# A top-2 expert dispatch on one core: one store fewer at the start, other load sizes, and a last store of the first half cut in two

## The chip, the cores and the metric

The kernel runs on one core of a Trainium2 chip. The metric is the device time of one execution in microseconds (us), the median of several runs. TensorE does nothing here. Four parts of the core matter: VectorE (DVE in the profile), ScalarE (ACT), the 16 DMA engines that carry all data between HBM and the on-chip memory, and SyncE (SP), which issues DMAs in program order and waits for semaphores before it does. ScalarE can issue DMAs too, on a queue of its own.

## The reference

There are 16 x 1024 = 16384 tokens with 512 float32 values each, and 8 router logits for each token. A softmax over the logits, its two largest values, and a division of these two by their sum give two weights a token; the output is the token's row times each weight.

```python
probs = probs / np.sum(probs, axis=-1, keepdims=True)
topk_indices = np.argsort(probs, axis=-1)[..., -k:]
topk_probs = np.take_along_axis(probs, topk_indices, axis=-1)
topk_probs = topk_probs / np.sum(topk_probs, axis=-1, keepdims=True)
x_expanded = x[:, :, np.newaxis, :].repeat(k, axis=2)
return (x_expanded * topk_probs[..., np.newaxis]).astype(np.float32)
```

So 33.6 MB of x are read and 67.1 MB are written. With two experts the weights are the sigmoids of plus and minus the difference of the two largest logits, and the kernel computes them so.

## The kernel before

Each of the 128 partitions holds M = 128 tokens, called rows here; one row in all partitions is 128 x 512 x 4 bytes = 262,144 bytes to load, and twice that, two half-rows, to store. The rows are worked in two groups of 65 and 63 (`GROUPS`, L16). `xs` has room for 65 rows of x. `osp` (`OSP`, L38) has room for 18 rows of output; its last three rows serve first as the place of the logits and as scratch for `top2_weights` (L41 to L68).

For each group the kernel issues its loads from SP (L111, L112) in the sizes of `LOADS` (L20): 6, 28 and 31 rows, then 32 and 31. Behind the first load, of 6 rows, come the two small loads of logits (L105, L106), and the weights of all rows are computed once, on DVE and with two sigmoids on ACT (L67, L68), into `WA`.

Then come the stores of the group, from `STORES` (L23 to L37). An entry gives the number of rows, where the output rows are built, how many of them ACT computes, and the queue. DVE multiplies most rows in one instruction (L127), which reads each row of x once for each of its two weights; ACT does the others, one activation a half-row (L135). When all are done the entry's DMA is issued (L138). An output row is built in `osp`, or in `xs` itself, over rows of x that are used up. "x", 2 means that the 16 output rows lie over xs rows 2 to 33, while they are computed from rows 18 to 33, in ascending order, so that no row is overwritten before it is read.

What sets the order is therefore this. SP has one list: the loads of the first group (group 0 in the code), its stores as they come ready, then the loads of the second group, and the second group's stores. A DMA that reads or writes rows that another piece of work still uses waits for it, and so does everything behind it on SP. The first load of the second group fills xs rows 0 to 31, the second one rows 32 to 62; each waits for the stores of group 0 that still read those rows. Before the change the stores of the first group are these: 2 rows from `osp` issued from ACT's queue as soon as the first 6 rows and the weights are there ("the early store"); 16 rows from `osp`; 16 rows from xs rows 2 to 33; 16 rows from `osp` again, which waits until the earlier `osp` store has landed; 15 rows from xs rows 35 to 64. The first load of the second group has no row in common with the last of these.

```python
            {"SP": nc.sync, "ACT": nc.scalar}[queue].dma_start(o_v[g][:, r : r + n], og)
```

In the texts below the loads are called A (6 rows), B, C (first group) and D, E (second group); the four stores of 15 to 17 rows of the first group are S0 to S3 in the order of the list, those of the second group T0 to T3.

Of the kernel before, what the change touches and what calls it, by code (L numbers as in the profile page):

```python
# [1 line left out]

# [4 lines left out]

F32 = mybir.dt.float32
ALU = mybir.AluOpType
ACTF = mybir.ActivationFunctionType  # L10
P = 128
E = 8
D = 512


GROUPS = [65, 63]  # L16
M = sum(GROUPS)


LOADS = [[6, 28, 31], [32, 31]]  # L20


STORES = [  # L23
    [
        (2, ("osp", 0), 0, "ACT"),
        (16, ("osp", 2), 0, "SP"),
        (16, ("x", 2), 0, "SP"),
        (16, ("osp", 0), 4, "SP"),
        (15, ("x", 35), 0, "SP"),
    ],  # L30
    [
        (16, ("osp", 0), 1, "SP"),
        (16, ("x", 0), 0, "SP"),
        (16, ("osp", 0), 4, "SP"),
        (15, ("x", 33), 0, "SP"),
    ],
]  # L37
OSP = 18  # L38


def top2_weights(nc, scratch, logits, WA):  # L41

    used = [0]

    def cut(n):
        a = scratch[:, used[0] : used[0] + M * n].rearrange("p (m n) -> p m n", n=n)
        used[0] += M * n
        return a

    a, b = logits[:, :, 0:4], logits[:, :, 4:8]  # L50
    hi = cut(4)
    lo = b
    nc.vector.tensor_tensor(hi, a, b, op=ALU.max)  # L53
    nc.vector.tensor_tensor(lo, a, b, op=ALU.min)  # L54
    n = 4
    while n > 1:
        n //= 2
        a, b = hi[:, :, 0:n], hi[:, :, n : 2 * n]
        nhi, nlo, tmp = cut(n), cut(n), cut(n)
        nc.vector.tensor_tensor(tmp, lo[:, :, 0:n], lo[:, :, n : 2 * n], op=ALU.max)  # L60
        nc.vector.tensor_tensor(nlo, a, b, op=ALU.min)  # L61
        nc.vector.tensor_tensor(nlo, nlo, tmp, op=ALU.max)  # L62
        nc.vector.tensor_tensor(nhi, a, b, op=ALU.max)  # L63
        hi, lo = nhi, nlo
    dlt = cut(1)
    nc.vector.tensor_tensor(dlt, hi, lo, op=ALU.subtract)  # L66
    nc.scalar.activation(WA[:, :, 0], dlt[:, :, 0], ACTF.Sigmoid, scale=-1.0)  # L67
    nc.scalar.activation(WA[:, :, 1], dlt[:, :, 0], ACTF.Sigmoid, scale=1.0)  # L68


@with_exitstack
def kernel(
    ctx: ExitStack,
    tc: tile.TileContext,
    x: bass.AP,
    router_logits: bass.AP,
    k: bass.AP,
    out: bass.AP,
):
    nc = tc.nc  # L80
    N = x.shape[0] * x.shape[1]
    assert int(k) == 2 and router_logits.shape[-1] == E and x.shape[2] == D
    assert N == P * M
    xf = x.rearrange("b s d -> (b s) d")
    of = out.rearrange("b s k d -> (b s) k d")
    rf = router_logits.rearrange("b s e -> (b s) e")
    x_v, o_v, rl_v = [], [], []
    t0 = 0
    for n in GROUPS:
        t1 = t0 + P * n  # L90
        x_v.append(xf[t0:t1].rearrange("(p m) d -> p m d", p=P))
        o_v.append(of[t0:t1].rearrange("(p m) k d -> p m k d", p=P))
        rl_v.append(rf[t0:t1].rearrange("(p m) e -> p m e", p=P))
        t0 = t1

    pool = ctx.enter_context(tc.tile_pool(name="pool", bufs=1))
    xs = pool.tile([P, max(GROUPS), D], F32)
    osp = pool.tile([P, OSP, 2, D], F32)
    WA = pool.tile([P, M, 2], F32)

    logits = osp[:, OSP - 1].rearrange("p k d -> p (k d)").rearrange("p (m e) -> p m e", e=E)
    scratch = osp[:, OSP - 3 : OSP - 1].rearrange("p r k d -> p (r k d)")

    def load_logits():
        nc.sync.dma_start(logits[:, : GROUPS[0]], rl_v[0])  # L105
        nc.sync.dma_start(logits[:, GROUPS[0] :], rl_v[1])  # L106

    m0 = 0
    for g, G in enumerate(GROUPS):
        r = 0  # L110
        for n in LOADS[g]:  # L111
            nc.sync.dma_start(xs[:, r : r + n, :], x_v[g][:, r : r + n, :])  # L112
            if g == 0 and r < 6 <= r + n:
                load_logits()
                top2_weights(nc, scratch, logits, WA)
            r += n
        assert r == G
        r = 0
        for n, (home, a), by_act, queue in STORES[g]:
            if home == "x":  # L120
                og = xs[:, a : a + 2 * n, :].rearrange("p (r k) d -> p r k d", k=2)
            else:
                og = osp[:, a : a + n]
            v = n - by_act
            w = WA[:, m0 + r : m0 + r + n, :]
            if v:
                nc.vector.tensor_tensor(  # L127
                    og[:, :v],
                    xs[:, r : r + v, :].unsqueeze(2).to_broadcast([P, v, 2, D]),
                    w[:, :v].unsqueeze(3).to_broadcast([P, v, 2, D]),  # L130
                    op=ALU.mult,
                )
            for i in range(v, n):
                for c in range(2):
                    nc.scalar.activation(  # L135
                        og[:, i, c], xs[:, r + i, :], ACTF.Copy, scale=w[:, i, c : c + 1]
                    )
            {"SP": nc.sync, "ACT": nc.scalar}[queue].dma_start(o_v[g][:, r : r + n], og)  # L138
            r += n
        assert r == G  # L140
        m0 += G


# [1 line left out]
_INS = ['x', 'router_logits', 'k']  # L145
_OUTS = [((16, 1024, 2, 512), 'float32')]

_NUMBERS = {'k': 2}


# [26 lines left out]
```

## Time and profile before

| what | value |
|---|---|
| median of 3 runs | 239.16 us (239.15 to 239.52) |
| the profiled execution, its own time | 239.38 us |
| its span, first to last instruction | 237.6 us |
| DVE busy | 132.2 us, 56% |
| ACT busy | 13.2 us, 6% |
| bytes by DMA | 101.19 MB, mean 426 GB/s over the span |

The span is what the trace covers; 1.8 us of the execution lie outside of it. A row of the page with 40 digits cuts the span in 40 slices of 5.94 us; a digit is the busy share of a slice in tenths, and the row named DMA is the mean of the 16 DMA engines. In the view of windows the last two numbers of a row are the DMA share and the GB/s. Both count a transfer's packet where it starts, with its whole length and all its bytes, so a short window can show more than 1.00, and the quotient of the two columns, the rate while busy, says more than either. "SPq" and "ACTq" are instructions of the engines' queues: an issue, not the transfer. The "us to landing" of an issue runs from its issue to its completion and so holds the time that it stood behind earlier transfers.

### The profile page before, as it was taken

What the parts mean: (1) busy time and instruction counts of PE and PEld (TensorE: products, weight loads), DVE (VectorE), ACT (ScalarE), POOL (GpSimd) and SP (SyncE); (2) the same over time, 40 slices, a digit from 0 to 9 for tenths busy, and PEclk for the clock granted to TensorE, in tenths of its full rate; (3) what the DMA queues carried; (4) which work ended last, traced back from release to release, by engine and by line L of the source; (5) the groups of instructions that cost most, each with busy time, mean ns of one, the idle gap of its engine ahead of it and who ended that gap; (6) DMA issues with size and microseconds to landing.
All of it is one profiled execution on the core that took longest, in us unless ns stands there. A gap on an engine that the chain in (4) does not pass through costs nothing.

```text
span 237.6 us, 124 instructions
## 1 busy us (share of the span) xinstructions
DVE 132.2 (56%) x20; ACT 13.2 (6%) x21; POOL 0.2 (0%) x4
## 2 busy tenths in 40 slices
DVE  0640599999289999000000009999956999920000
ACT  2000000000080000000000001000006100000000
POOL 0000000000000000000000000000000000000000
DMA  7979989898989989899998989898989989897995
GB/s 265 541 338 488 408 386 535 348 530 353 496 386 441 441 353 530 353 508 414 414 519 353 508 370 502 353 519 353 496 386 419 463 353 530 353 530 342 496 445 217
DMA packets 2304, 101.19 MB, mean 426 GB/s; under 512 B 256, under 2 KB 384, under 8 KB 512
## 3 DMA queue, kind: packets, MB, share of 16 engines
q1 hardware_dynamic: 2160, 100.14, 97.7%
q10 hardware_dynamic: 144, 1.05, 1.0%
HBM read 34.08 MB, written 67.11 MB: 426 GB/s over the span
## 4 chain that ended last, share of the span: by engine, by line
DMA 48%; DVE 39%; SPq 1%; issue 0%; DVEq 0%
DMA xs<-in_x_dram 30%; DVE osp L127 25%; DMA out_dram<-osp 19%; DVE xs L127 14%; SPq L105 0%; SPq L106 0%; SPq L112 0%; SPq L138 0%; DVEq L127 0%
## 5 line engine op out<-in xcount | busy, mean ns | idle before, releaser
L127 DVE TENSOR_TENSOR osp<-xs,WA 128x12288 f32<-128x12288 f32 (+3 forms) x5 | 61.6, 12318 | 68.7 <-DMA xs<-in_x_dram 58.4
L127 DVE TENSOR_TENSOR xs<-xs,WA 128x16384 f32<-128x16384 f32 (+1 forms) x4 | 66.8, 16692 | 0.3
L135 ACT ACTIVATE osp<-xs,WA 128x512 f32<-128x512 f32 x18 | 11.4, 709 | 161.3 <-DMA out_dram<-osp 90.0
L53 DVE TENSOR_TENSOR osp<-osp 128x512 f32<-128x512 f32 x1 | 0.7, 692 | 8.2 <-DMA osp<-in_router_logits_dram 8.2
L67 ACT ACT_TABLE_LOAD x1 | 1.3, 1283 | 0.7 <-PEq L158 0.7
L67 ACT ACTIVATE WA<-osp 128x128 f32<-128x128 f32 x1 | 0.3, 316 | 10.1 <-DVE osp L66 10.1
L54 DVE TENSOR_TENSOR osp<-osp 128x512 f32<-128x512 f32 x1 | 0.7, 693 | 0.0
L60 DVE TENSOR_TENSOR osp<-osp 128x256 f32<-128x256 f32 (+1 forms) x2 | 0.7, 352 | 0.0
L62 DVE TENSOR_TENSOR osp<-osp 128x256 f32<-128x256 f32 (+1 forms) x2 | 0.7, 352 | 0.0
L63 DVE TENSOR_TENSOR osp<-osp 128x256 f32<-128x256 f32 (+1 forms) x2 | 0.7, 352 | 0.0
L61 DVE TENSOR_TENSOR osp<-osp 128x256 f32<-128x256 f32 (+1 forms) x2 | 0.7, 351 | 0.0
L66 DVE TENSOR_TENSOR osp<-osp 128x128 f32<-128x128 f32 x1 | 0.3, 292 | 0.0
L68 ACT ACTIVATE WA<-osp 128x128 f32<-128x128 f32 x1 | 0.3, 298 | 0.0
L158 POOL MEMSET const-bfloat16-1.0<- 128x1 bf16 x1 | 0.1, 102 | 0.0
L158 POOL MEMSET const-uint8-127<- 128x1 uint8 x1 | 0.1, 102 | 0.0
L158 POOL MEMSET const-float32-0.0<- 128x1 f32 x1 | 0.1, 99 | 0.2 <-issue 0.2
L158 POOL MEMSET const-float32-1.0<- 128x1 f32 x1 | 0.1, 99 | 0.0
## 6 DMA issues: line engine op xcount, KB each, us to landing
xs<-in_x_dram SPq DMA_DIRECT2D x2, 7936.0 KB, 40.8
out_dram<-xs SPq DMA_DIRECT2D x2, 7680.0 KB, 27.5
xs<-in_x_dram SPq DMA_DIRECT2D x1, 7168.0 KB, 24.2
xs<-in_x_dram SPq DMA_DIRECT2D x1, 1536.0 KB, 6.0
out_dram<-osp ACTq DMA_DIRECT2D x1, 1024.0 KB, 24.5
osp<-in_router_logits_dram SPq DMA_DIRECT2D x1, 260.0 KB, 6.2
osp<-in_router_logits_dram SPq DMA_DIRECT2D x1, 252.0 KB, 6.4
out_dram<-osp SPq DMA_DIRECT2D x4, 23.9
```

Source lines behind the costliest of these rows:

```text
L53: nc.vector.tensor_tensor(hi, a, b, op=ALU.max)
L54: nc.vector.tensor_tensor(lo, a, b, op=ALU.min)
L60: nc.vector.tensor_tensor(tmp, lo[:, :, 0:n], lo[:, :, n : 2 * n], op=ALU.max)
L61: nc.vector.tensor_tensor(nlo, a, b, op=ALU.min)
L62: nc.vector.tensor_tensor(nlo, nlo, tmp, op=ALU.max)
L63: nc.vector.tensor_tensor(nhi, a, b, op=ALU.max)
L66: nc.vector.tensor_tensor(dlt, hi, lo, op=ALU.subtract)
L67: nc.scalar.activation(WA[:, :, 0], dlt[:, :, 0], ACTF.Sigmoid, scale=-1.0)
L68: nc.scalar.activation(WA[:, :, 1], dlt[:, :, 0], ACTF.Sigmoid, scale=1.0)
L127: nc.vector.tensor_tensor(og[:, :v], xs[:, r : r + v, :].unsqueeze(2).to_broadcast([P, v, 2, D]), w[:, :v].unsqueeze(3).to_broadcast([P, v ...
L135: nc.scalar.activation(og[:, i, c], xs[:, r + i, :], ACTF.Copy, scale=w[:, i, c : c + 1])
L158: nc = _bacc.Bacc("TRN2", target_bir_lowering=False, num_devices=1)
```

## The change

The early store is gone from the list, and with it the entry for ACT's queue. The loads of the first group are 6, 29 and 30 rows. An entry of `LOADS` now also names the xs row where it begins (the same as before by running count), and an entry of `STORES` the xs row from which its rows are computed. The stores of the first group are 16, 16, 16 and 17 rows. S0 is built in `osp` from row 0 of it, with 2 rows by ACT; S1 over xs rows 0 to 31, from rows 16 to 31; S2 in `osp`, as the third store before; S3, 17 rows computed from xs rows 48 to 64, 4 of them by ACT, over xs rows 14 to 47. S3's DMA is cut in two: the first 29 half-rows (xs rows 14 to 42) and the last 5 (xs rows 43 to 47). The first load of the second group, rows 0 to 31, now has rows in common with S1 and with the first part of S3; the second load, rows 32 to 62, with both parts. The second group's tables are the same as before.

```diff
-LOADS = [[6, 28, 31], [32, 31]]
+LOADS = [[(6, 0), (29, 6), (30, 35)], [(32, 0), (31, 32)]]
 STORES = [
     [
-        (2, ("osp", 0), 0, "ACT"),
-        (16, ("osp", 2), 0, "SP"),
-        (16, ("x", 2), 0, "SP"),
-        (16, ("osp", 0), 4, "SP"),
-        (15, ("x", 35), 0, "SP"),
+        (16, 0, ("osp", 0), 2, "SP", 0),
+        (16, 16, ("x", 0), 0, "SP", 0),
+        (16, 32, ("osp", 0), 4, "SP", 0),
+        (17, 48, ("x", 14), 4, "SP", 5),
     ],
...
-        for n, (home, a), by_act, queue in STORES[g]:
+        for n, s, (home, a), by_act, queue, cut in STORES[g]:
...
-                    xs[:, r : r + v, :].unsqueeze(2).to_broadcast([P, v, 2, D]),
+                    xs[:, s : s + v, :].unsqueeze(2).to_broadcast([P, v, 2, D]),
...
-            {"SP": nc.sync, "ACT": nc.scalar}[queue].dma_start(o_v[g][:, r : r + n], og)
+            src = og.rearrange("p m k d -> p (m k) d")
+            dst = o_v[g][:, r : r + n].rearrange("p m k d -> p (m k) d")
+            for c0, c1 in ((0, 2 * n - cut), (2 * n - cut, 2 * n)):
+                if c0 < c1:
+                    {"SP": nc.sync, "ACT": nc.scalar}[queue].dma_start(
+                        dst[:, c0:c1], src[:, c0:c1]
+                    )
```

More of the change, by code (lines that the diff above doesn't have):

```diff
@@ L17 @@
 M = sum(GROUPS)
-LOADS = [[6, 28, 31], [32, 31]]
+LOADS = [[(6, 0), (29, 6), (30, 35)], [(32, 0), (31, 32)]]
 STORES = [
     [
-        (2, ("osp", 0), 0, "ACT"),
-        (16, ("osp", 2), 0, "SP"),
-        (16, ("x", 2), 0, "SP"),
-        (16, ("osp", 0), 4, "SP"),
-        (15, ("x", 35), 0, "SP"),
-    ],
-    [
[L32 to L35, printed above, removed]
+        (16, 0, ("osp", 0), 2, "SP", 0),
+        (16, 16, ("x", 0), 0, "SP", 0),
+        (16, 32, ("osp", 0), 4, "SP", 0),
+        (17, 48, ("x", 14), 4, "SP", 5),
+    ],
+    [
+        (16, 0, ("osp", 0), 1, "SP", 0),
+        (16, 16, ("x", 0), 0, "SP", 0),
+        (16, 32, ("osp", 0), 4, "SP", 0),
+        (15, 48, ("x", 33), 0, "SP", 0),
     ],
@@ L110 @@
         r = 0
-        for n in LOADS[g]:
-            nc.sync.dma_start(xs[:, r : r + n, :], x_v[g][:, r : r + n, :])
+        for n, s in LOADS[g]:
+            nc.sync.dma_start(xs[:, s : s + n, :], x_v[g][:, r : r + n, :])
             if g == 0 and r < 6 <= r + n:
@@ L135 @@
                     nc.scalar.activation(
-                        og[:, i, c], xs[:, r + i, :], ACTF.Copy, scale=w[:, i, c : c + 1]
+                        og[:, i, c], xs[:, s + i, :], ACTF.Copy, scale=w[:, i, c : c + 1]
                     )
-            {"SP": nc.sync, "ACT": nc.scalar}[queue].dma_start(o_v[g][:, r : r + n], og)
+            src = og.rearrange("p m k d -> p (m k) d")
[5 more added lines that the diff above has]
+                    )
             r += n
```

## The prediction, made before the changed kernel ran

> **What bounds the kernel now.** I read the page first, for who is busy.
>
> ```profile
> span 237.6 us, 124 instructions
> DVE  0640599999289999000000009999956999920000
> DMA  7979989898989989899998989898989989897995
> q1 hardware_dynamic: 2160, 100.14, 97.7%
> q10 hardware_dynamic: 144, 1.05, 1.0%
> ```
>
> DVE rests for long stretches; the DMA engines never do. Their packets fill 97.7% + 1.0% of 16 engines' span. SP's queue is q1; q10 is ACT's, which carries the early store alone (1.05 MB). A kernel so bound can gain only where the stream is late, empty or slowed. To find such places I read the view of windows, over the start and then over steady stretches.
>
> ```profile
> 0.00:1.74 1.74, 0.00 (x0) 1.01 (x1) 0.20 (x4) 1.00 0.00 0
> 1.74:2.40 0.66, 0.00 (x0) 0.27 (x1) 0.00 (x0) 1.00 1.43 298
> 9.25:17.60 8.35, 5.06 (x11) 0.51 (x2) 0.00 (x0) 1.00 1.01 440
> 17.60:22.20 4.60, 0.00 (x0) 0.00 (x0) 0.00 (x0) 1.00 1.00 427
> 22.20:25.10 2.90, 0.00 (x0) 0.00 (x0) 0.00 (x0) 1.00 0.94 362
> 25.10:45.60 20.50, 19.21 (x2) 0.00 (x0) 0.00 (x0) 1.00 1.01 435
> 104.00:141.30 37.30, 0.00 (x0) 0.00 (x0) 0.00 (x0) 1.00 0.99 430
> ```
>
> The quotient of the last two columns is the rate while busy: 440/1.01 = 436, 435/1.01 = 431 and 430/0.99 = 434 GB/s, but 427/1.00 = 427 between 17.60 and 22.20 and 362/0.94 = 385 between 22.20 and 25.10. Two decimals make such a quotient good to half a per cent, and 385 lies far outside of that: the stream is slowed there, after the early store's issue at 14.95. Landings give a sharper rate: the chain of waits and the issues.
>
> ```profile
> 2.10 24.16 DMA xs<-in_x_dram
> ...
> 43.61 22.22 DMA out_dram<-osp
> ...
> 95.18 0.02 issue
> ...
> 95.58 46.42 DMA xs<-in_x_dram
> ...
> 158.32 21.80 DMA out_dram<-osp
> ```
>
> ```profile
> osp<-in_router_logits_dram SPq DMA_DIRECT2D x1, 252.0 KB, 6.4
> out_dram<-xs SPq DMA_DIRECT2D x1, 7680.0 KB, 27.7
> out_dram<-xs SPq DMA_DIRECT2D x1, 7680.0 KB, 27.3
> ```
>
> B lands at 2.10 + 24.16 = 26.26, S0 at 43.61 + 22.22 = 65.83, load D at 95.58 + 46.42 = 142.00, T0 at 158.32 + 21.80 = 180.12. Between S0's and D's landings lie S1, S2, S3 and D: 3 x 8.389 + 7.864 = 33.03 MB in 76.17 us (a row of x is 0.2621 MB to load, 0.5243 to store), **433.6 GB/s**, or 0.4336 MB a us. Between D's and T0's lie E and T0: 8.126 + 8.389 = 16.52 MB at 433.6 is 38.09, measured 38.12. So nothing is lost from 65.83 on.
>
> **The change part by part.** I need the order in time:
>
> ```profile
> 1.64 0.42 SPq L106 DMA_DIRECT2D osp<-in_router_logits_dram  x1
> 14.95 0.37 ACTq L138 DMA_DIRECT2D out_dram<-osp  x1
> 26.35 17.23 DVE L127 TENSOR_TENSOR osp<-xs,WA 128x16384 f32<-128x16384 f32 x1 [11.43 <-DMA xs<-in_x_dram]
> 43.61 0.35 SPq L138 DMA_DIRECT2D out_dram<-osp  x1
> 65.95 12.96 DVE L127 TENSOR_TENSOR osp<-xs,WA 128x12288 f32<-128x12288 f32 x1 [5.11 <-DMA out_dram<-osp]
> 79.01 16.16 DVE L127 TENSOR_TENSOR xs<-xs,WA 128x15360 f32<-128x15360 f32 x1
> 95.20 0.33 SPq L138 DMA_DIRECT2D out_dram<-xs  x1
> 95.58 27.65 SPq L112 DMA_DIRECT2D xs<-in_x_dram  x2
> 209.45 0.33 SPq L138 DMA_DIRECT2D out_dram<-xs  x1
> ```
>
> *The early store goes.* Its bytes don't go: S3 has 17 rows for 15, and S0 to S3 now carry all 65. What goes is what it costs beside its bytes. The logits land at 1.64 + 6.4 = 8.04; from there to S0's landing at 65.83 are 57.79 us, in which B (7.340 MB), C (8.126), the early store (1.049) and S0 (8.389) pass, 24.90 MB, which at 433.6 take 57.43. That is **0.36 us lost**, in the only stretch in which two queues carry data. The windows agree: 17.60 to 22.20 holds 4.60 x 427/433.6 = 4.53 us of work in 1.00 x 4.60, 0.07 lost; 22.20 to 25.10 holds 2.90 x 362/433.6 = 2.42 in 0.94 x 2.90 = 2.73, 0.31 lost. The early store (issue 14.95, behind packets under way) begins to move in these windows, as the row of its queue for 17.60 to 25.10 shows:
>
> ```profile
> q1 hardware_dynamic: 48, 2.75, 89.5%
> q10 hardware_dynamic: 32, 0.26, 8.2%
> ```
>
> Window 9.25 to 17.60, with the same load B and no packet of q10, shows no loss. So I take -0.36. Bounds: the loss could belong to B's end and stay (0), or, with the tenths of the q10 row (1.0% of 237.6 is 2.38 us for bytes that take 2.42, +-0.12) and the spread between engines, reach -0.6.
>
> *Two rows less for DVE ahead of load B's rows.* DVE idled 11.43 us before S0; the removed instruction lay ahead of that wait. Nothing.
>
> *Loads of 6, 29 and 30 rows.* The stream decides when they land. B lands at 8.04 + 7.602 MB at that rate (17.53 us) = 25.57, C 18.14 later at 43.71. S0 needs A and B. DVE starts 0.09 after (26.35 in the old row, where B landed at 26.26) and has 14 rows: between 12.96 for 12 and 16.16 for 15, 1.07 a row, so 15.09. ACT's 2 rows, 4 activations of 5.01/8 = 0.63 each (row below), lie beside it. SP issues S0 at 40.78.
>
> ```profile
> 65.94 5.01 ACT L135 ACTIVATE osp<-xs,WA 128x512 f32<-128x512 f32 x8 [53.34 <-DMA out_dram<-osp]
> ```
>
> S0's issue is then 2.93 ahead of C's landing. Before, it was issued at 43.61 and C landed 19.35 us (S0's bytes) before 65.83, at 46.48: 2.87 ahead, and the windows show no gap there. The cover is unchanged: nothing.
>
> *S0 to S2.* S0 lands at 43.71 + 19.35 = 63.06, S1 at 82.41, S2 at 101.76. DVE ends S1 at 40.8 + 17.2 = 58.0, 5 ahead of S0's landing. S2 waits for S0's landing as the old third store does (63.06 + 0.12 + 12.96 = 76.1, 6 ahead of S1's). Nothing.
>
> *S3's new wait.* It writes xs rows 14 to 47, and S1 reads rows 14 to 31: DVE must wait for S1's landing, 82.41 + 0.12. It computes 13 rows, 14.02: S3's first part is issued at 96.6, 5.2 ahead of S2's landing. Nothing is behind this instruction on DVE but T0, which needs D. ACT's 8 activations take 5.0, beside it. A start of the stream on an empty queue takes 1.01 to 1.67 (issue at 0.73; first packets from 1.74, all 16 by 2.40: 298 x 0.66 is 16 packets of 12,288 bytes), so some 3 us of cover are left over. Nothing.
>
> *D's new wait*, the place where it is decided. On SP, D stands behind S3's two DMAs' issues and waits for the first part's landing; E and T0 to T3 stand behind it. The first part, 29 half-rows, 7.602 MB, lands at 101.76 + 17.53 = 119.29; meanwhile the second, 5 half-rows, 1.311 MB, drains: 3.02 us of cover. What it must cover:
>
> ```profile
> DMA packets 16, 0.00 MB, mean 0 GB/s; under 512 B 16, under 2 KB 16, under 8 KB 16
> DMA packets 32, 1.05 MB, mean 2622 GB/s; under 512 B 16, under 2 KB 16, under 8 KB 16
> ```
>
> The first row is the DMA view of 235.97 to 236.38: 16 tiny packets, by which the 16 engines end the last store, 0.41 apart. It lands at 209.45 + 27.3 = 236.75, 0.4 after the last. The second is 121.84 to 122.24, the old S3's 16 (with D's first large packets); it lands at 95.20 + 27.7 = 122.9, 0.66 after. Then SP's reaction, 0.02 (the issue row at 95.18), and 1.01 to 1.67 to the first packets; and the first packets in the stretch 1.74:2.40 took 1.43 x 0.66 = 0.94 where 12,288 bytes at the rate take 0.45: 0.49 more. Sum 1.9 to 2.8, after the slowest engine's end. The fastest engine is 0.41 ahead, so its cover is 3.02 - 0.41 = 2.6, the slowest's 3.02. **Bubble: 0 to 0.2**, and I take 0, since only the longest of each term together reach it.
>
> The Trainium skill speaks against this one: "DMA: Bandwidth & Descriptors", section "Anatomy of one DMA — SWDGE (gpsimd) path", puts a fixed cost of about 2.0 us on a DMA, most of it the receipt of the write, heaviest for HBM. With 2.0 for the landing the sum would be 3.5 to 4.2 and the bubble 0.5 to 1.6. The two landings above, 0.4 and 0.66, disagree with it; no landing right ahead of a small store is in this trace.
>
> *E* waits for the second part, which lands at 122.3; D is then in flight for 19 us more. Nothing. Before, E stood in the same way for S3, from D's issue until 122.9, as the queue's own waits have it:
>
> ```profile
> SPq L112 <- DMA out_dram<-xs: 26.2, 1, 26.2
> ```
>
> The second part costs one issue, 0.35, and bytes that are counted.
>
> **Sum**: D lands at 122.31 + 19.35 = 141.66 against 142.00, and group 2's order is the old one, so all that follows moves with it. -0.36 + 0: the span goes to 237.25, the profiled execution from 239.38 to 239.02. The median lies 0.22 under the profiled one; the same step takes 239.16 to **238.8**.
>
> **The rivals.**
>
> *The bubble before D decides.* If a landing among stores, or the restart, takes longer than the rows say, each us beyond 2.6 is lost whole, since nothing else is queued. It gives 239.16 - 0.36 + b: from 3.0 the gain is gone, and from 2.6 + 0.84 = 3.4 the kernel is slower by over 0.2%; with a landing of 1.5, somewhat over twice the longest row, and the start's worst, 3.7, b is 1.1 and the time 239.9. For: no wait of before stands so close to the stream's end; 26.2 us of wait on the old S3 had D's 8.4 MB as cover. Against: the rows.
>
> *The loss isn't the early store's*, but that of B's end, where loads of C follow. Then it stays: 239.2. For: the largest part falls on B's last packets. Against: D's end, where loads of E follow, costs nothing (65.83 to 142.00 to 180.12 above). A rule of the Trainium skill goes with this rival: the same page, "Issuing engines are not separate DMA queues", says that DMAs of all issuers run on the same 16 engines and interleave, a second queue saving only issue time; by it a second queue's presence costs no rate. The 385 GB/s above doesn't decide it.
>
> *More is freed*: engines differ, and the slowest sets every landing; at -0.6, 238.6.
>
> *It doesn't do what it says*: D waits for both parts of S3, or S3 misses its slot. The queue then runs dry, 1.9 to 2.8 us: 240.7 to 241.6. Against: the old D was issued at 95.58 with S3 in flight on other rows of `xs`, while E waited; so waits go by rows.
>
> **How the numbers follow.** Forecast 0.50 (its own range 238.6 to 239.0, of which 0.22 lies under 238.68); more freed 0.10; loss not the early store's 0.14; bubble 0.20, of which 0.12 over 0.2%; wrong wait or slot 0.06. About 0.2%, 0.48 us, is what a measurement of this kernel can tell from no change: faster is under 238.68, slower over 239.64. Faster 0.22 + 0.10 = 0.32; slower 0.12 + 0.06 = 0.18; within 0.50. The range leaves out the wrong wait and the bubbles over 0.9 (0.15) and little below: 238.4 to 239.7.
>
> **What would show it.** Right: rate while busy about 434 from 9.25 to 25; DVE's first L127 at 25.7; S0's issue at 40.8; S3's DVE start at 82.5 after a DMA; D's issue at 119.3, with a full DMA share from 119 to 123; D's landing at 141.7. Wrong: a D landing later than its 19.35 us after the second part's; 385 GB/s again before 25; or an issue of D at 122.3.

## The result, and the profile after

The changed kernel takes 240.54 us in the median of 8 runs (239.78 to 241.14) against 239.26 (239.15 to 239.52) before: slower, ratio 1.0048 with a 95% interval of 1.0032 to 1.0065. Its runs spread over 1.36 us, those of the kernel before over 0.37. The profiled execution took 241.14, the slowest of the eight, with a span of 239.4.

The page of the changed kernel, the rows shown of before:

```profile
span 239.4 us, 138 instructions
DMA  7979979998989898998999999988989898998994
q1 hardware_dynamic: 2304, 101.19, 98.1%
```

One queue carries all, as many bytes as before, and nearly as dense. Windows first, the three over the start and four later ones, with DMA share and GB/s at the end:

```profile
9.25:17.60 8.35, 2.77 (x10) 0.51 (x2) 0.00 (x0) 1.00 1.05 455
17.60:22.20 4.60, 0.00 (x0) 0.00 (x0) 0.00 (x0) 1.00 0.95 413
22.20:25.10 2.90, 0.00 (x0) 0.00 (x0) 0.00 (x0) 1.00 1.49 645
...
121.50:121.95 0.45, 0.00 (x0) 0.00 (x0) 0.00 (x0) 1.00 5.62 2207
121.95:124.00 2.05, 0.00 (x0) 0.00 (x0) 0.00 (x0) 1.00 0.11 32
160.10:160.90 0.80, 0.79 (x1) 0.00 (x0) 0.00 (x0) 1.00 0.00 0
160.90:161.10 0.20, 0.20 (x1) 0.00 (x0) 0.00 (x0) 1.00 11.50 4915
```

The start does what was forecast: 455/1.05, 413/0.95 and 645/1.49 are 433 to 435 GB/s, and the 385 of before is gone. In 160.10 to 160.90 no packet begins; the next ones begin in a bunch. For the first time since the start of either trace the queue was dry. The chain of waits says why:

```profile
58.17 24.31 DMA out_dram<-xs
...
96.66 22.67 DMA out_dram<-xs
...
119.34 24.33 DMA xs<-in_x_dram
...
143.86 16.17 DVE osp L129
...
160.10 21.71 DMA out_dram<-osp
```

D, issued at 119.34, lands at 119.34 + 24.33 = 143.67, 2.0 after the forecast; T0, computed from it, is issued at 160.10, when most engines have finished E. What delayed D is in the DMA view of 121.50 to 123.50, where a slot is 0.05 us, and in the row of its queue for 122.88 to 123.50:

```profile
DMA  9999909900000000000000000009000000000000
GB/s 4137 6554 3932 1311 1311 0 1311 1311 0 0 0 0 0 0 0 0 0 0 0 0 0 0 0 0 0 0 0 1311 0 0 0 0 0 0 0 0 0 0 0 0
DMA packets 33, 1.06 MB, mean 529 GB/s; under 512 B 16, under 2 KB 16, under 8 KB 16
...
q1 hardware_dynamic: 1, 0.07, 35.6%
```

Each 1311 is one packet of 65,536 bytes, the first of D on one engine (the first three slots hold eleven, and the last short packet of S3). Fifteen engines go from S3 to D within 0.4 us; the sixteenth begins 1 us after the last of them, at 122.88, and its first packet takes 0.356 x 0.62 x 16 = 3.5 us where 65,536 bytes at the rate take 2.4. That is 2.1 in all, about the 2.0 by which D lands late. The landing comes with the slowest engine: fifteen have ended D by 141.73, the last at 143.32. So the fifteen gain nothing by being early, and since nothing else was queued after E, they ran dry waiting for T0.

### The profile page after: what moved, and what is told of

Read it like the earlier page. It is cut to its first block, busy times and chain, and to the rows that moved or that the text cites. A ratio compares the mean times of both kernels' runs of the same rounds, so it can differ in the third digit from the quotient of the medians.

```text
span 239.4 us, 138 instructions
## 1 busy us (share of the span) xinstructions
DVE 125.6 (52%) x19; ACT 20.7 (9%) x33; POOL 0.2 (0%) x4
## 4 chain that ended last, share of the span: by engine, by line
DMA 49%; DVE 38%; SPq 1%; issue 0%; DVEq 0%
DMA xs<-in_x_dram 20%; DVE xs L129 20%; DMA out_dram<-xs 20%; DVE osp L129 18%; DMA out_dram<-osp 9%; SPq L107 0%; SPq L108 0%; SPq L114 0%; DVEq L129 0%; SPq L144 0%
## 5 line engine op out<-in xcount | busy, mean ns | idle before, releaser
L129 DVE TENSOR_TENSOR osp<-xs,WA 128x12288 f32<-128x12288 f32 (+2 forms) x4 | 57.2, 14292 | 70.5 <-DMA xs<-in_x_dram 60.9
L129 DVE TENSOR_TENSOR xs<-xs,WA 128x16384 f32<-128x16384 f32 (+2 forms) x4 | 64.6, 16158 | 6.7 <-DMA out_dram<-xs 6.4
L137 ACT ACTIVATE osp<-xs,WA 128x512 f32<-128x512 f32 x22 | 13.9, 710 | 149.9 <-DMA xs<-in_x_dram 78.1
L137 ACT ACTIVATE xs<-xs,WA 128x512 f32<-128x512 f32 x8 | 5.1, 710 | 5.5 <-DVE osp L129 5.5
```

Source lines behind the costliest of these rows:

```text
L129: nc.vector.tensor_tensor(og[:, :v], xs[:, s : s + v, :].unsqueeze(2).to_broadcast([P, v, 2, D]), w[:, :v].unsqueeze(3).to_broadcast([P, v ...
L137: nc.scalar.activation(og[:, i, c], xs[:, s + i, :], ACTF.Copy, scale=w[:, i, c : c + 1])
```

## The experiments

After the logits' landing the stream lost time in two places only, in all 20 profiles: before S0's landing, and from there to D's landing. From D's landing to T0's it never lost more than 0.11. So each profile gives two losses, worked out from its landings as the prediction does: from the logits' landing to S0's, and from S0's to D's, each less the bytes between at 0.4336 MB a us. "S0 ahead" is S0's issue before C's landing, that without a delay at C's own end; the expectations below count to C's end on the first engine, some 0.8 less. Where the early store runs on ACT's queue, "lost to S0" holds its own loss near 22 us (0.34 before the change) beside that at C's end. Each profile is one run; where runs spread, it is one of that spread. Those of after, e2 and g2 are the longest of their kernels, k1's the second longest, those of f1 and f2 the shortest, so the losses shown for the former are on the high side, those of f1 and f2 on the low one.

| kernel | early store | S3's second part, if D waits | S0 ahead | lost to S0 | lost S0 to D | median (lowest to highest) |
|---|---|---|---|---|---|---|
| before | ACT | no wait | 2.9 | 0.34 | 0.00 | 239.16 to 239.33 in six sets of runs |
| after | no | 5 half-rows | 2.8 | 0.02 | 1.98 | 240.54 (239.78 to 241.14) |
| e1 | no | 16 | 2.8 | 0.00 | 1.32 | 239.64 (239.13 to 241.15) |
| e2 | no | no wait | 2.8 | 0.05 | 2.30 | 240.78 (240.01 to 241.47) |
| e3 | SP, behind C | no wait | 29 (early store) | 1.03 | 0.05 | 240.25 (240.02 to 240.36) |
| e4 | no | none | 2.8 | -0.02 | 2.69 | 242.08 (241.96 to 242.62) |
| f1 | no | no wait | 2.8 | 0.08 | 0.31 | 240.81 (240.60 to 240.96), 1.2 of it two more rows |
| f2 | no | no wait | 3.4 | 0.48 | 0.00 | 239.84 (239.56 to 240.11) |
| f3 | ACT | 5 | 2.9 | 0.09 | 0.76 | 239.74 (239.32 to 240.72) |
| f4 | no | no wait | 2.8 | 0.17 | 0.93 | 240.49 (239.31 to 241.06) |
| g1 | no | no wait | 2.4 | 0.08 | 1.73 | 241.03 (240.88 to 241.26) |
| g2 | ACT | no wait | 2.0 | 0.44 | 2.00 | 239.90 (239.66 to 241.43) |
| g3 | no | no wait | 2.4 | 0.18 | 1.99 | 241.15 (241.10 to 241.58) |
| g4 | no | no wait | 6.0 | 1.47 | -0.02 | 240.42 (240.21 to 240.64) |
| h1 | no | 5 | 3.8 | 0.91 | 0.57 | 240.26 (240.04 to 240.63) |
| h2 | no | 16 | 3.9 | 1.02 | -0.05 | 240.04 (240.00 to 240.22) |
| h3 | ACT | no wait | 3.0 | 0.35 | 0.18 | 239.35 (239.18 to 239.91) |
| h4 | ACT | no wait | 5.0 | 0.96 | -0.01 | 239.93 (239.90 to 239.98) |
| k1 | no | no wait | 2.8 | 0.05 | 1.94 | 240.49 (239.31 to 241.29) |
| k2 | no | 16 | 3.4 | 0.21 | 0.39 | 239.88 (239.60 to 240.67) |

The first theory after the result was the prediction's own rival: **cover too short**. D's new wait leaves 3.0 us of stores in the queue, and on the slowest engine the way from S3's first part to D's data takes longer. Rivals: the wait as such, or the cut with its short packets.

### e1: a longer second part

```diff
-        (17, 48, ("x", 14), 4, "SP", 5),
+        (17, 48, ("x", 14), 4, "SP", 16),
```

> The last 16 half-rows of S3 form the second part instead of 5, so that 9.7 us of stores stand in the queue while D waits for the first part's landing (18 half-rows), instead of 3.0. Theory 'cover too short': on the slowest DMA engine the way from the first part's end to D's data takes about 5 us (118.84 to 124.0 in the changed kernel's trace), which 9.7 hides: 238.9 (238.7 to 239.1). Rival 'the wait itself': a load issued on a store's landing leaves one engine behind whatever stands in front of it: 240.5 as the changed kernel. Rival 'the cut': short packets set an engine back; 32 KB packets for 10 KB would leave a part of it, 239.2 to 240.

239.64 (ratio to before 1.0027, 1.0009 to 1.0044), in two heaps: six runs from 239.13 to 239.34, six from 239.95 to 241.15. The longer second part helps, and in the better heap the kernel is level with the one before. But five runs still lose a us and more, with three times the cover: the theory explains a part. The median lies in the range of the rival "the cut", which the next run takes away together with the wait.

### e2: no wait at all

```diff
-        (16, 0, ("osp", 0), 2, "SP", 0),
-        (16, 16, ("x", 0), 0, "SP", 0),
-        (16, 32, ("osp", 0), 4, "SP", 0),
-        (17, 48, ("x", 14), 4, "SP", 5),
+        (17, 0, ("osp", 0), 3, "SP", 0),
+        (16, 17, ("x", 0), 0, "SP", 0),
+        (16, 33, ("osp", 0), 4, "SP", 0),
+        (16, 49, ("x", 33), 0, "SP", 0),
```

> The changed kernel with the first group's stores as 17, 16, 16 and 16 rows, S3 over xs rows 33 to 64 and not cut: D has no row in common with S3 and is issued right behind it, as before the change; the early store stays away. All three theories on D say no lag: D's landing 0.3 to 0.4 before that of the kernel before, and 238.9 if the early store's loss of 0.36 was its own; 239.3, as before, if that loss has another cause.

240.78 (1.0062, 1.0047 to 1.0076): slower than before by more than the changed kernel, though D is issued at 95.17, as before the change. All three theories on D fall as the whole cause. Something that the early store or its place in the order did is missing.

### e3: the early store on the other queue

```diff
-        (2, ("osp", 0), 0, "ACT"),
+        (2, ("osp", 0), 0, "SP"),
```

> The kernel before with one word changed: the early store of 2 rows is issued from SP's queue instead of ACT's, so that it runs behind load C and one queue carries everything. If the 0.36 us between 17.6 and 25.1 are the cost of two queues at once, they go: 238.9. If they belong to the end of load B, they stay: 239.3.

240.25 (1.0038, 1.0025 to 1.0051), neither of the two. The loss near 22 us goes, as the first theory said, but the last packets of C, now followed at once by a store that has waited since 15.1, lose 1.03, and D starts free of loss. By the Trainium skill ("DMA: Bandwidth & Descriptors", "Issuing engines are not separate DMA queues") a second queue saves issue time only; here the queue also decides what a transfer runs beside, and that is 1 us.

### e4: no cover

```diff
-        (17, 48, ("x", 14), 4, "SP", 5),
+        (17, 48, ("x", 14), 4, "SP", 0),
```

> The changed kernel without the cut: S3's 34 half-rows are one transfer and D waits for all of it, with nothing behind. 'Cover too short': the whole way lies bare, 0.5 to landing, 1 to 1.7 to the first packets, 0.5 more for their data on most engines (2 to 2.8), and up to 5 on the slowest: 241 to 244, the slow engine again one alone. 'The cut' as cause of the slow engine: all engines restart within some 0.6 us of each other, 240.9 to 241.7. 'The wait itself': as the first.

242.08 (1.0121, 1.0107 to 1.0134). Its windows after S3's last byte:

```profile
121.97:123.30 1.33, 0.00 (x0) 0.00 (x0) 0.00 (x0) 1.00 0.00 0
123.30:124.10 0.80, 0.00 (x0) 0.00 (x0) 0.00 (x0) 1.00 4.03 1311
```

1.33 us without a packet, then all 16 engines' first packets within 0.8 us (1311 x 0.80 is 16 x 65,536 bytes), on average 4.03 x 0.80 = 3.2 long where 65,536 bytes at the rate take 2.4. The loss, 2.69, lies within the 1.9 to 2.8 that the prediction had worked out for a bare wait: landing 0.35, issue 0.02, first packets 1.0 to 1.8 later, then slow first packets. No engine is late alone. The estimate of the wait's chain was right; the wait just isn't all that matters.

### f1: everything 1.2 us later

On most engines of the changed kernel and of e2, D's first packets ended as if they had begun at 121.7 to 122.1 (their end less the 2.4 us of the steady rate), though S3 ended at different times. Was it the time that mattered ("instant"), or the turn from stores to loads? f1 is e2 with two rows of x loaded twice (into rows that C fills later, so that C's issue waits for them, until 9.29).

```diff
                 load_logits()
+                nc.sync.dma_start(xs[:, 40:42, :], x_v[0][:, 0:2, :])
```

> The kernel of e2 with one load more in front of load B (2 rows read a second time, 0.52 MB, 1.2 us of the stream); everything behind it comes 1.2 us later. In e2 and in the changed kernel, D's first data come at 121.7 to 122.1 on nearly all engines, though the stores in front end up to 0.4 earlier, and one engine follows 1 to 2.5 late. Theory 'instant': something holds D's reads until about 121.9 after the start, whatever the stream does; here S3 ends at 122.6 or later, so no engine lags, and the time is that of e2 without its lag and with 1.2 more, about 240.1, in a narrow spread. Theory 'turn': the change from stores to loads costs what it costs in the absence of the early store; then an engine lags again, 241.5 to 242.

240.81, or 239.6 without the 1.2. It fits neither. No engine lagged alone in this profile, against "turn"; but 0.31 was lost to D, and the time is 0.7 above the 240.1 of "instant". What that theory can't hold is g2 below. Its DMA view of 122.38 to 122.98 holds the 16 tiny packets by which the engines end S3:

```profile
DMA packets 31, 0.98 MB, mean 1639 GB/s; under 512 B 16, under 2 KB 16, under 8 KB 16
```

That is well after 121.9, and D still loses 2.00. Why f1's runs are so much better than e2's, the runs don't settle.

### f2, f4: the early store alone, and S3's size

f2 is the kernel before without the early store, its rows put into S0; f4 is e2 with S3 of 15 rows.

```diff
-        (2, ("osp", 0), 0, "ACT"),
-        (16, ("osp", 2), 0, "SP"),
+        (18, ("osp", 0), 4, "SP"),
```

> The kernel before with the early store's 2 rows put into S0 (18 rows in osp, 4 of them by ACT) and nothing else changed: loads 6, 28, 31, S1 to S3 and D as before. Theory 'turn without the early store': D lags as in e2, 240 to 241.5. Theory 'size of S3' (15 rows here, 16 or cut in the kernels that lag): no lag, 238.9. Theory 'instant': S3 ends at 121.4 to 121.9, so an engine lags, 240 to 241.

```diff
-        (16, 17, ("x", 0), 0, "SP", 0),
-        (16, 33, ("osp", 0), 4, "SP", 0),
-        (16, 49, ("x", 33), 0, "SP", 0),
+        (17, 17, ("x", 0), 0, "SP", 0),
+        (16, 34, ("osp", 0), 4, "SP", 0),
+        (15, 50, ("x", 35), 0, "SP", 0),
```

> The kernel of e2 with one row moved from S3 to S1 (17, 17, 16, 15): S3 is 15 rows as in the kernel before, and the stream is else as in e2. Theory 'size of S3': no lag, 238.9. Theories 'turn without the early store' and 'instant': an engine lags, 240 to 241.5.

f2 took 239.84 (1.0026, 1.0016 to 1.0035), with its loss at C's end (0.48) and none up to D. f4 took 240.49 (1.0045, 1.0024 to 1.0067), with its loss at D. So an S3 of 15 rows doesn't keep D's start free. The early store gone costs 0.6, not -0.36, and the loss has two possible places.

### f3: the wait alone

```diff
-        (2, ("osp", 0), 0, "ACT"),
-        (16, ("osp", 2), 0, "SP"),
-        (16, ("x", 2), 0, "SP"),
-        (16, ("osp", 0), 4, "SP"),
-        (15, ("x", 35), 0, "SP"),
+        (2, 0, ("osp", 0), 0, "ACT", 0),
+        (16, 2, ("osp", 2), 0, "SP", 0),
+        (16, 18, ("x", 2), 0, "SP", 0),
+        (16, 34, ("osp", 0), 4, "SP", 0),
+        (15, 50, ("x", 18), 0, "SP", 5),
```

> The kernel before, early store, loads and sizes kept, with S3 built over xs rows 18 to 47 and cut so that D waits for its first 25 half-rows, while 5 drain: the change's wait alone. Theory 'cover too short': an engine lags, 240.5 to 241. Theories 'turn without the early store' and 'instant' (S3 ends at 121.9 to 122.3): no lag, 239.3, as the kernel before.

239.74 (1.0025, 1.0013 to 1.0038): between the two. With early store, loads and sizes as before, the wait behind 3.0 us of cover, together with the cut that makes it, costs 0.5 in the median and up to 1.5. No run has the cut without the wait.

### g1 to g4: how early S0 is issued

Laid side by side, the profiles showed that the place of the loss went with how far S0's issue lay ahead of C's end. g1 and g4 move S0's issue by ACT's share of its rows, g2 is the change's loads alone, g3 e2 with the old loads.

```diff
 g1, on f2
-        (18, ("osp", 0), 4, "SP"),
+        (18, ("osp", 0), 3, "SP"),
 g2, on the kernel before
-LOADS = [[6, 28, 31], [32, 31]]
+LOADS = [[6, 29, 30], [32, 31]]
 g3, on e2
-LOADS = [[(6, 0), (29, 6), (30, 35)], [(32, 0), (31, 32)]]
+LOADS = [[(6, 0), (28, 6), (31, 34)], [(32, 0), (31, 32)]]
-        (17, 0, ("osp", 0), 3, "SP", 0),
+        (17, 0, ("osp", 0), 2, "SP", 0),
 g4, on e2
-        (17, 0, ("osp", 0), 3, "SP", 0),
+        (17, 0, ("osp", 0), 6, "SP", 0),
```

> The kernel of f2 (early store merged into S0, all else as before) with 3 of S0's rows by ACT instead of 4, so that DVE takes 1.07 us longer and S0 is issued at 41.3 instead of 40.3, some 1.7 ahead of load C's end instead of 2.8. In f2's trace the last packets of C run 0.45 longer on nearly all engines, in the changed kernel (S0 issued 2.2 ahead) they don't. Theory 'queued too early': that cost goes, 239.84 becomes 239.4 or, with the early store's 0.36, down to 238.9. Theory 'split rows' (S0's 18 rows travel as two packets a partition): the cost stays, 239.8.

> The kernel before with loads of 6, 29 and 30 rows instead of 6, 28 and 31 and nothing else changed: the change's loads alone. All theories: 239.2 to 239.3, as before; a lag of an engine behind S3 would say that the loads alone bring it.

> The kernel of e2 (no early store, 17, 16, 16, 16 rows, D without a wait) with the old loads 6, 28 and 31; S0 has 2 rows by ACT, so that it is issued at 41.3. Theory 'phase' (two of the engines are set back when they run in step, which a disturbance at the end of C would spread, and here is none): an engine lags, 240 to 241.5, as e2. Theory 'loads': no lag, 239.3 or less.

> The kernel of e2 with 6 of S0's rows by ACT instead of 3: S0 is issued at 37.7 instead of 40.9, 5 us ahead of C's end. Theory 'queued too early': C's last packets take 0.5 to 1.1 longer on all engines. Theory 'phase': with that, no engine lags behind S3, and the time is 239.5 to 240.1 in a narrow spread instead of 240 to 241.5; without it, the lag stays on top, 241 to 242.

g1: 241.03 (1.0080, 1.0067 to 1.0093). C's end is free of loss, as "queued too early" said, but the kernel is 1.2 slower than f2: the loss is at D, and larger. g2: 239.90 (1.0039, 1.0025 to 1.0053), missed by every theory; its S0 comes 1 us later, since B has one row more. g3: 241.15 (1.0086, 1.0073 to 1.0099), with its loss at D. g4: 240.42 (1.0052, 1.0038 to 1.0065), 0.3 over what "phase" expected, with its loss at C's end alone, in a spread of 0.43. Two rows for each of three kernels show it: windows that hold the 16 engines' last packets of C, and of S3, with the rate while busy as the quotient of the last two columns. Before:

```profile
43.35:43.85 0.50, 0.47 (x2) 0.00 (x0) 0.00 (x0) 1.00 4.68 2032
119.50:120.00 0.50, 0.00 (x0) 0.00 (x0) 0.00 (x0) 1.00 4.59 1966
```

g4, S0 6.0 ahead (15 of the 16 packets of S3):

```profile
40.54:40.97 0.43, 0.43 (x1) 0.00 (x0) 0.00 (x0) 1.00 8.18 2286
120.00:120.60 0.60, 0.00 (x0) 0.00 (x0) 0.00 (x0) 1.00 3.78 1638
```

g2, S0 2.0 ahead:

```profile
43.10:44.00 0.90, 0.90 (x1) 0.00 (x0) 0.00 (x0) 1.00 2.52 1092
119.45:120.15 0.70, 0.00 (x0) 0.00 (x0) 0.00 (x0) 1.00 4.25 1404
```

Before, 434 and 428: next to nothing at either turn. g4, 279 and 433: a packet at C's end takes 8.18 x 0.43 = 3.5 on average instead of 2.3, and D begins free. g2, 433 and 330: the reverse. New theory, **lead**: S0 queued far ahead of C's end costs about 1 us there and spares D's start; S0 queued late does the opposite.

### h1 to h4: S0's lead moved by itself

```diff
 h1, on the changed kernel, and h2, on e1
-        (16, 0, ("osp", 0), 2, "SP", 0),
+        (16, 0, ("osp", 0), 3, "SP", 0),
 h3, on g2
-        (16, ("osp", 2), 0, "SP"),
+        (16, ("osp", 2), 1, "SP"),
 h4, on the kernel before
-        (16, ("osp", 2), 0, "SP"),
+        (16, ("osp", 2), 2, "SP"),
```

> The changed kernel with 3 of S0's rows by ACT instead of 2: S0 is issued 1.07 us earlier, 3.1 ahead of C's end instead of 2.06; wait, cut and sizes stay. Theory 'lead': C's last packets take some 0.7 longer on all engines, D begins with hardly a loss and without a lagging engine: 239.4 to 239.8 in a narrow spread. Rival 'cover too short': D's loss stays, 240.5, or 241 with C's on top.

> The kernel of e1 (second part of S3 of 16 half-rows) with the same edit: S0 issued 3.1 ahead of C's end instead of 1.9. Theory 'lead': the runs at 239.9 to 241.2 vanish, all lie at 239.3 to 239.8. Rival 'chance, whatever the lead': two heaps again, 239.2 and 240 to 241.

> The kernel of g2 (before, with loads 6, 29, 30; S0 1.07 ahead of C's end; 239.9, up to 241.4) with 1 of S0's rows by ACT, so that S0 is issued 2.1 ahead as in the kernel before. Theory 'lead': 239.2 to 239.4 and no lag, the loads as such cost nothing. Rival 'loads': 239.9 with runs at 241, as g2.

> The kernel before with 2 of S0's rows by ACT: S0 is issued 2.1 us earlier, 4.3 ahead of C's end instead of 2.1, and nothing else changes. Theory 'lead': C's last packets take about 1 us longer on all engines: 240.0 to 240.4, in a narrow spread. Rival 'S0 earlier costs nothing': 239.2, as DVE's and ACT's work is hidden behind the loads either way.

h4: 239.93 (1.0033, 1.0021 to 1.0045), all runs within 0.08. An edit that only moves 2 of 16 rows from DVE to an idle ACT costs 0.8 us, since it makes S0 ready earlier. h3: 239.35 (1.0007, 0.9998 to 1.0016): the loads alone cost nothing once S0 is issued as far ahead as before. h2: 240.04, 0.2 over the expected range, but all within 0.22, where e1 had two heaps over 2.0. h1: 240.26, 0.5 over the expected range; the loss at C's end came (0.91), but 0.57 stayed at D. h1 differs from h2 by the length of S3's second part alone, and of its 0.57 h2 shows nothing. So the lead is a cause and the short second part another. The length sets two things, the cover (3.0 or 9.7 us) and the size of the packets (10,240 or 32,768 bytes); which of the two it is, no run tells. The windows of C's last packets in h2, and of a part of S3's second part:

```profile
40.52:41.05 0.53, 0.53 (x1) 0.00 (x0) 0.00 (x0) 1.00 6.05 1855
120.30:121.20 0.90, 0.00 (x0) 0.00 (x0) 0.00 (x0) 1.00 0.67 291
```

307 and 434 GB/s: the loss is all at C's end.

### k1, k2: the early store's own part, and the cheapest point without it

```diff
 k1, on f2
-LOADS = [[6, 28, 31], [32, 31]]
+LOADS = [[6, 29, 30], [32, 31]]
 k2, on e1
-LOADS = [[(6, 0), (29, 6), (30, 35)], [(32, 0), (31, 32)]]
+LOADS = [[(6, 0), (28, 6), (31, 34)], [(32, 0), (31, 32)]]
```

> The kernel of f2 (early store merged into S0, S1 to S3 and D as before) with loads 6, 29, 30, which brings S0's issue to 2.0 ahead of C's end, as in the kernel before (2.1). Theory 'lead alone': nothing at C's end and hardly anything at D's start, 238.9 to 239.3. Theory 'the early store keeps D's start free': a loss of 0.3 or more at D's start, with lagging engines in some runs: 239.3 to 241.

> The kernel of e1 (no early store, second part of S3 of 16 half-rows, lead 1.9) with loads 6, 28, 31, so that S0 is issued 2.6 ahead of C's end. Theory 'lead': C's end costs about 0.45, D's start little, no second heap: 239.2 to 239.6, narrower than e1 (239.13 to 241.15). It beats the kernel before only if both losses stay under 0.3.

k1: 240.49 (1.0041, 1.0023 to 1.0058), eight of twelve runs over 240, in the range of "the early store keeps D's start free"; h3, which has the early store and nearly the same lead (3.0 for 2.8), had none over 239.91. The windows over C's and S3's last packets, first k1, then h3:

```profile
40.40:41.20 0.80, 0.70 (x2) 0.00 (x0) 0.00 (x0) 1.00 2.84 1229
119.15:119.75 0.60, 0.00 (x0) 0.00 (x0) 0.00 (x0) 1.00 4.65 1638
```

```profile
43.10:43.90 0.80, 0.69 (x2) 0.00 (x0) 0.00 (x0) 1.00 2.83 1229
119.30:119.95 0.65, 0.00 (x0) 0.00 (x0) 0.00 (x0) 1.00 3.66 1512
```

k1: 433 and 352 GB/s, free at C's end, slowed at D. h3: 434 and 413, nearly free at both. The kernel before, at 2.9, loses nothing at D. So a lead of some 2.8 to 3.0 is not enough by itself; with the early store it is. k1's S0 has 18 rows for h3's 16, but that is hardly the difference: e1, with 16 rows, k1's lead and 9.7 us of cover, is slow in half of its runs and loses 1.32 at D in its profile, and f2, with 18 rows and a lead of 3.4, loses nothing there. k2: 239.88 (1.0022, 1.0011 to 1.0033), 0.3 over the expected range, with a little lost at both places. No kernel tried beats the one before. (In k1's and k2's set the kernel before had a median of 239.33 and one run of 23 at 240.58, so it isn't quite immune.)

## Why the prediction was wrong

**The timetable up to D was right.** Forecast and measured: B lands at 25.57, 25.60; S0 is issued at 40.78, 40.90, and lands at 63.06, 63.09; S1 82.41, 82.48; S2 101.76, 101.80; S3's first part 119.29, 119.32, its second 122.31, 122.45; D is issued at 119.31, 119.34. DVE's and ACT's new waits cost nothing, as said. The 0.36 us was real: lost to S0 went from 0.34 to 0.02, and S3 ended 0.42 earlier than before. Yet 240.54 stands against a forecast of 238.8, and the profile has 1.98 lost between S0's and D's landings, where the forecast had 0 to 0.2.

**The first failing step is "What goes is what it costs beside its bytes."** It booked the early store's 0.36 us as a gain by taking it for the only thing that the early store did. k1 against h3 shows what else: without it, at nearly the same lead of S0 and without any new wait, D's start loses 1.94 in the profile instead of 0.18, and the median is 1.16 above that of the kernel before in the same set, instead of 0.19. The early store pays 0.36 near 22 us and spares more at 120. The prediction's check that "nothing is lost from 65.83 on" was true of the kernel before and was carried over to one in which its condition was gone.

**The second is "Bubble: 0 to 0.2".** The chain was sized rightly for an empty queue (e4), but a bubble was the wrong picture: the queue needn't run empty for D's start to lose. The wait with its short second part has a price: 0.5 in the median where it is the only change (f3), and 0.9 less in the median where the part is lengthened (e1). The two prices don't add up, since they fall on the same place: wait and removal together cost 1.28, the removal with the loads 1.16 (k1), the wait 0.5.

**The third is that S0's cover was taken as one-sided.** The prediction asked whether S0 is issued early enough, found 2.93 and 2.87 ahead, and put nothing down. For C's end that was right (0.02 lost to S0), but by luck of the sizes: in the kernel before, 1 us later or 2 earlier costs 0.7 to 0.8 (g2, h4).

Of the rivals, the bubble before D named the place and the sign, with 0.20, and gave 239.9 for a bubble of 1.1; the measured loss was larger and only partly the wait's. "The loss isn't the early store's" was wrong. One of the signs named, a D landing later than 19.35 after the second part's, is what came: 143.67 - 122.45 is 21.22. The rule of the Trainium skill that spoke against the change, a fixed cost of about 2.0 us for a DMA ("DMA: Bandwidth & Descriptors", "Anatomy of one DMA — SWDGE (gpsimd) path"), which that section gives for DMAs issued by GpSimd and not by SP or ACT, would have put the bubble at 0.5 to 1.6, nearer to what came; but not for its reason: the landing after the last packet took 0.5 (118.84 to 119.32) in the changed kernel, not 2.0.

What stays open is the mechanism inside the DMA engines. The runs show a trade between the two turns of the stream and its dependence on S0's lead and on the early store, not what an engine does there. Also open: why in some of the profiles that lose at D a single engine falls back (after, e1, g2) and in others four or five (f3, f4, g3, k1), which no run settles, and why f1 loses less than e2.

## What to carry to other kernels

In a stream that is bound by DMA, the places to look at are its turns, from loads to stores and back: measure the loss at each in the kernel as it is, before pricing an edit anywhere ahead of them. A transfer that seems to cost something may be what keeps a later turn cheap, so take it away alone, with everything else in place, before a bigger change is built on its absence. And "ready earlier" isn't free for a store: when the median moves by less than the spread of the runs, look at the spread, since a second heap shows a cause that one profile can miss.

## What the runs showed of the hardware that was not expected

- From D's landing to T0's, a load and then a store of 16.5 MB together, the stream moves 433.6 GB/s in every kernel, to about 0.1 us in 38. The turn between them, with T0 issued 2.3 to 2.6 us ahead of E's landing, costs no more than that.
- A store that waits in the queue well before the loads in front of it end slows their last packets, on all engines from 3.8 us on: the mean excess of C's last packets over their time at the rate is 0.36 (k2) and 0.44 (f2) with the store issued 3.4 ahead, 0.84 and 0.94 at 3.8 and 3.9 (h1, h2), 0.69 at 5.0 (h4, which has the early store), 1.25 at 6.0 (g4) and 1.14 at 29 (e3); next to nothing at 2.0 to 3.0.
- One of the 16 engines can fall back by 1 us and more on its own and stays last to the end of the kernel, and every landing waits for it. In the changed kernel it ends D 1.6 after the fifteenth, and, once the others have waited for T0, the last store still 0.8 after it.
- A dry queue restarts in 0.8 to 1.0 us (T0's issue at 160.10, first packets after 160.90; in e4 D's issue at 122.34, first packets after 123.30).
